# A width-31 depthwise convolution on TensorE: 8 time phases by 16 channels in the partitions instead of 4 by 32

## Chip, cores and metric

One Trainium2 chip, all 8 cores, one batch element per core. The time is the device time in microseconds (us) of the slowest core. In some executions the cores of one die show a lower granted clock (0.89 to 0.92 on one die in a run of 853.56 us) and the whole run is some per cent longer; such slow runs are left out of all comparisons. "Control" below means the kernel before, unaltered, run beside the experiments. "Core mean" is the mean of the eight core spans over the fast runs; it scatters less than the slowest core.

## The reference, cut to what matters

```python
D_MODEL = 1024; BATCH = 8; SEQ = 2048; CFM_K = 31        # FFN_HIDDEN = 2816
# per sequence: x (2048, 1024) f32, conditioning vector c (1024)
h  = modulate(rmsnorm(x, g_pre_mix), sh1, sc1)            # sh, sc, gt from silu(c) @ w_ada
gb, gc, v, a, g = split(h @ w_in, 5)                      # 512 columns each
y_short = gb * causal_dwconv(gc * v, w_short, b_short)    # width 3
u = a * sigmoid(g)                                        # (S, 512)
u = causal_dwconv(u, w_cfm_dw, b_cfm_dw)                  # depthwise, width 31   <- the change
u = layernorm(u, g_cfm_ln, b_cfm_ln)                      # over the 512 channels
y_cfm = silu(u)
y = per_head_rmsnorm(concat(y_short, y_cfm)) * beta_mix   # heads of 64 channels
x = x + gt1 * rmsnorm(y @ w_out, g_post_mix)              # output projection
x = x + gt2 * rmsnorm(swiglu(modulate(rmsnorm(x), ...)), g_post_ffn)
```

## The kernel before

The program records every operation with an estimated cost; a static scheduler then fixes the order of each engine's instructions before the run. So an engine executes in that order, even if a DMA comes later than planned and other work would be ready.

The depthwise convolution would waste TensorE if each channel had its own row of weights only. So the 128 partitions hold 32 channels times 4 time phases (position t has phase t mod 4). One 128 x 128 tap matrix then mixes all phases of a channel, and 31 taps need only 9 shifts of the phase-decimated sequence. VectorE builds the tap matrices from a table `wv` and a mask `dlt`.

```python
NPH = 4; CH = S // NPH; NG = 16; NTAP = 9; HALO = 32; URow = HALO + CH
cw_s = sb_space("cw", 4, NTAP * 128, BF16, at=xc_off)     # room for tap matrices built ahead
junk_s = sb_space("junk", 1, D, BF16)                     # scratch: squares nobody reads
xq = x_d.rearrange("(b p q) d -> q b p d", p=128, q=NPH)  # token tiles: every 4th row
...
def norm_cast(xt, i, dst):
    act(Tile(junk_s).v(), xt, AF.Square, ..., accum=sm(SM_SSQ + i), name="pn_sq")
    rsqrt_col(i, "pn_rs")                                 # two small GpSimd instructions
    return dve("tensor_scalar", ..., out=dst, in0=xt, scalar1=sm(SM_RS + i), op0=ALU.mult)
...
for g in range(NG):                                       # the convolution stage
    cw = Tile(cw_s)
    dve("tensor_tensor", ..., name "cwm")                 # 1152 elements a partition
    b = bank('mm', *B05)
    for s in range(NTAP):
        o = s * 128
        u0 = g * URow + HALO - s
        mm(b.v(), cw.v(o, o + 128), up.v(u0, u0 + CH), s == 0, s == NTAP - 1, name="conv")
    uv = u1.v(g * CH, g * CH + CH)
    act(uv, b.v(), AF.Identity, bias=..., name="cv_ev")
    act(s1, b.v(), AF.Square, bias=..., name="cv_sq")
    dve("tensor_copy", [uv], [s0], ...)                   # cast to bf16
    mm(km.v(), ones_ln.v(), s0, ...); mm(kq.v(), ones_ln.v(), s1, ...)   # LayerNorm sums
    if g % 2 == 1 and g >= 3 and g < 11: ada_cols(6 + (g - 3) // 2, ...) # conditioning pieces
    ...
def outproj(q, pairs):                                    # output projection, quarter q
    for b in range(4):
        xt = Tile(xc_s).v()                               # 4 buffers: load x, add, store x1
        dma("pool", [(xt, xq[q, b])], [], [xt], 1.35, "xload2")
        ...                                               # 16 matmuls of 512 into a PSUM pair
        post(pt.v(), xt, 0, 16 + i)                       # gate, Square into junk, root, add
        dma("sp", [(x1q[q, b], xt)], [xt], ..., "x1st")
        xb_ = Tile(xn_s)
        last = norm_cast(xt, 32 + i, xb_.v())
    to_hT(xns, q, 1, last, (6, 7))                        # transposes for the FFN
```

Of the kernel before, what the change touches and what calls it, by code (L numbers as in the profile page):

```python
# [7 lines left out]
F32 = mybir.dt.float32  # L8
BF16 = mybir.dt.bfloat16
# [9 lines left out]
NPH = 4  # L19
CH = S // NPH  # L20
NG = 16
NTAP = 9
HALO = 32
URow = HALO + CH
# [439 lines left out]
def build_program():  # L464
# [17 lines left out]
    with es:  # L482
# [24 lines left out]
        u1 = buf("u1", NG * CH, F32)  # L507
        up = buf("up", NG * URow, BF16)
        stg_s = sb_space("stg", 4, CH, BF16)
        dg3 = buf("dg3", 12 * 128, BF16)  # L510
        end_stg = cur[0]
        cvb = [buf("cvb%d" % i, 4 * URow, BF16, at=up.off + i * 8 * URow) for i in range(4)]
# [9 lines left out]
        cw_s = sb_space("cw", 4, NTAP * 128, BF16, at=xc_off)  # L522
        lnb = [buf("ln%d" % i, 512, F32, at=xc_off + 2048 * (5 + i)) for i in range(3)]
# [8 lines left out]
        junk_s = sb_space("junk", 1, D, BF16)  # L532
# [10 lines left out]
        wv = buf("wv", NW, BF16)  # L543
        dlt = buf("dlt", 32, BF16)
# [74 lines left out]
        def wload(src, n, name, sp=slot_s, split=1, **kw):  # L619
# [14 lines left out]
        dve("tensor_copy", [ident.v()], [sel.v()], 250, "c6", out=View(lambda: sel.v(0, 128, 0, 4).ap.rearrange("k (c p) -> k c p", p=4), []),  # L634
            in_=ident.t[0:4, 0:4].unsqueeze(1).to_broadcast([4, 32, 4]))
        mk = bank("tp", 6, 7)
        mm(mk.v(0, 128), sel.v(0, 128, 0, 4), sel.v(0, 128, 0, 4), True, True, n=128, name="mask")
        dve("tensor_scalar", [mk.v()], [ones_ln.v()], 250, "c7", out=ones_ln.t[:, :], in0=mk.v(0, 128), scalar1=1.0 / 512.0, scalar2=None, op0=ALU.mult)
        dve("tensor_scalar", [mk.v()], [blk32.v()], 250, "c7", out=blk32.t[:, :], in0=mk.v(0, 128), scalar1=1.0 / 64.0, scalar2=None, op0=ALU.mult)
        dve("tensor_tensor", [ident.v()], [dlt.v()], 150, "c7", out=dlt.t[:, :], in0=ident.t[:, 0:32], in1=ident.t[:, 32:64], op=ALU.add)  # L640
        for h in range(2, 4):
            dve("tensor_tensor", [ident.v(), dlt.v()], [dlt.v()], 150, "c7", out=dlt.t[:, :], in0=dlt.t[:, :], in1=ident.t[:, 32 * h:32 * h + 32], op=ALU.add)
# [24 lines left out]
        def ada_cols(piece, kind, l, half, banks, **kw):  # L667
            s = wload(wada_d[piece], 4096, "wada%d" % piece, **kw)
# [38 lines left out]

        xq = x_d.rearrange("(b p q) d -> q b p d", p=128, q=NPH)
        x1q = x1_d.rearrange("(b p q) d -> q b p d", p=128, q=NPH)
        oq = out_d.rearrange("(b p q) d -> q b p d", p=128, q=NPH)  # L710
# [7 lines left out]
        def norm_cast(xt, i, dst):  # L718
            act(Tile(junk_s).v(), xt, AF.Square, n=1024, scale=1.0 / 32.0, accum=sm(SM_SSQ + i), writes=[("ssq", i)], name="pn_sq")
            rsqrt_col(i, "pn_rs")  # L720
            return dve("tensor_scalar", [xt, ("rs", i)], [dst], 750, "pn_xn", out=dst, in0=xt, scalar1=sm(SM_RS + i), scalar2=None,
                       op0=ALU.mult)
# [73 lines left out]
        def glu(j, q, gv, av, late=""):  # L796
# [6 lines left out]
            for c in range(4):  # L803
                g = 4 * j + c
                wk += up.v(g * URow + HALO, g * URow + HALO + CH, 32 * q, 32 * q + 32).keys
            dv = upv[32 * q:32 * q + 32, 4 * j:4 * j + 4, HALO:HALO + CH]
            return dma("sp", [(dv, sv.v())], [sv.v()], [View(None, wk)], SHUF, "ushuf")
# [34 lines left out]
        for g in range(NG):  # L842
            cw = Tile(cw_s)
            ov = View(lambda cw=cw: cw.v().ap.rearrange("k (s c p) -> k s c p", s=NTAP, p=NPH), [])
            w3 = wv.t[:, g * NTAP * NPH:(g + 1) * NTAP * NPH].rearrange("k (s p) -> k s p", s=NTAP)
            dve("tensor_tensor", [wv.v(), dlt.v()], [cw.v()], 1300, "cwm", out=ov,
                in0=dlt.t[:, :].unsqueeze(1).unsqueeze(3).to_broadcast([128, NTAP, 32, NPH]),
                in1=w3.unsqueeze(2).to_broadcast([128, NTAP, 32, NPH]), op=ALU.mult)
            b = bank('mm', *B05)
            for s in range(NTAP):  # L850
                o = s * 128
                u0 = g * URow + HALO - s
                mm(b.v(), cw.v(o, o + 128), up.v(u0, u0 + CH), s == 0, s == NTAP - 1, name="conv")
            uv = u1.v(g * CH, g * CH + CH)
            act(uv, b.v(), AF.Identity, reads=[K_V], bias=vc(V_BCF + g), npt=1, name="cv_ev")
            s1 = Tile(sq_s).v()
            act(s1, b.v(), AF.Square, reads=[K_V], bias=vc(V_BCF + g), npt=1, name="cv_sq")
            s0 = Tile(sq_s).v()
            dve("tensor_copy", [uv], [s0], 430, "cv_bf", out=s0, in_=uv)
            mm(km.v(), ones_ln.v(), s0, g == 0, g == NG - 1, name="lnm")  # L860
            mm(kq.v(), ones_ln.v(), s1, g == 0, g == NG - 1, name="lnq")
            if g % 2 == 1 and g >= 3 and g < 11:
                ada_cols(6 + (g - 3) // 2, "sc" if g < 7 else "sh", 1, (g // 2 + 1) % 2, B05, split=4)
            elif g == 11:
                wb = wload(wb_d, 4096, "wb", split=4)
                rowb(0)
                rg0 = [rowg(0, half) for half in range(2)]
        mv, rv, m2 = tmean.v(), trstd.v(), lnb[2].v()
        act(mv, km.v(), AF.Copy, name="ln_m")
        dve("tensor_tensor", [mv], [m2], 690, "ln_m2", out=m2, in0=mv, in1=mv, op=ALU.mult)  # L870
        dve("tensor_tensor", [kq.v(), m2], [rv], 690, "ln_var", out=rv, in0=kq.v(), in1=m2, op=ALU.subtract)
        act(rv, rv, AF.Ln, reads=[("eps",)], bias=sm(SM_EPS), npt=1, name="ln_ln")
        act(rv, rv, AF.Exp, scale=-0.5, name="ln_exp")

        last_silu = [None]

        def ln(g):
            uv = u1.v(g * CH, g * CH + CH)
            dve("tensor_tensor", [uv, mv], [uv], 690, "ln_sub", out=uv, in0=uv, in1=mv, op=ALU.subtract)
            dve("tensor_tensor", [uv, rv], [uv], 690, "ln_mul", out=uv, in0=uv, in1=rv, op=ALU.mult)  # L880
            last_silu[0] = act(uv, uv, AF.Silu, reads=[K_V], bias=vc(V_BLN + g), scale=vc(V_GLN + g), npt=2, name="silu")

        def head_norm(h):
            st = pair('hd', 6)
            for h2 in range(2):
                for gg in range(2):
                    g = 2 * (h + h2) + gg
# [3 lines left out]
                    mm(st.v(h2 * 512, h2 * 512 + 512, part=h2), blk32.v(), s1, gg == 0, gg == 1, name="hdst")  # L891
# [3 lines left out]
            for h2 in range(2):  # L895
                for gg in range(2):
                    g = 2 * (h + h2) + gg
                    uv = u1.v(g * CH, g * CH + CH)
                    sv = Tile(ystg_s)
                    r2 = rr.v(h2 * 512, h2 * 512 + 512)  # L900
                    dve("scalar_tensor_tensor", [uv, r2, K_V], [sv.v()], 750, "hd_out", out=sv.v(), in0=uv, scalar=vc(V_BETC + g), in1=r2,
                        op0=ALU.mult, op1=ALU.mult)
# [5 lines left out]
                    dv = yT.t[32 * c:32 * c + 32, (4 + j) * S:(5 + j) * S].rearrange("c (p t) -> c p t", p=NPH)  # L908
                    dma("sp", [(dv, sv.v())], [sv.v()], [View(None, wk)], SHUF, "yshuf")

        behind = {i: [lambda g=g: ln(g) for g in range(2 * i, 2 * i + 2)] for i in range(8)}
        for i in range(4):
            behind[8 + 2 * i] = [lambda h=h: head_norm(h) for h in (2 * i,)]

        for i in range(4):
            hk = []
            for q in range(4):
# [249 lines left out]
```

## Time and profile before

| | kernel before |
|---|---|
| median of 4 runs | 803.19 us (one of the four slow) |
| profiled run | 801.97 us; core spans 789.9 to 800.4 us |
| TensorE busy, slowest core | 746.4 of 800.4 us |
| convolution stage | 42 us, all TensorE |

The profiled core shown is core 5, the slowest. The groups of the convolution by form, kernel before. Columns: line, engine, operation, output<-input with shapes, count, then busy us and mean ns of one, then idle time of that engine just before and what ended most of it:

```profile
L576 PE MATMUL ps<-up,cw 128*128 128x512 bf16 x144 | 33.9, 379 | 0.0
...
L592 DVE TENSOR_TENSOR cw<-dlt,wv 128x1152 bf16<-128x1152 bf16 x16 | 21.7, 1356 | 8.1 <-PE ps L576 8.1
...
L588 ACT ACTIVATE u<-ps,vt 128x512 f32<-128x512 f32 x16 | 11.0, 687 | 21.7 <-PE ps L576 21.7
```

TensorE has no idle time before its 144 convolution matmuls; VectorE and ScalarE wait for TensorE, not the other way round.

### The profile page before, as it was taken

How to read it: one execution, taken by the hardware profiler on the slowest of the kernel's cores; microseconds unless marked ns; L12 is line 12 of the kernel's file. 1: busy time of each engine (PE TensorE's matmuls, PEld its weight loads, DVE VectorE, ACT ScalarE, POOL GpSimd, SP SyncE). 2: the span in 40 equal slices, each digit the busy share in tenths (PEclk: the TensorE clock that was granted, in tenths of full speed). 3: DMA queues.
4: the chain of work that ended last, by engine and by line, in shares of the span. 5: the costliest groups of instructions: out<-in, count | busy, mean ns of one | idle time of the engine just before them, and what ended most of it. 6: DMA issues, size and time to landing. Idle time of an engine off the chain costs nothing.

```text
span 800.4 us, 10695 instructions; the slowest of 8 cores (789.9 to 800.4 us)
## 1 busy us (share of the span) xinstructions
PE 746.4 (93%) x3969; PEld 349.7 (44%) x3969; DVE 298.0 (37%) x429; ACT 261.0 (33%) x413; POOL 139.5 (17%) x275
## 2 busy tenths in 40 slices
PE   0788999999999989799999999999999999999993
PEld 0444444544444434354444444444444444444441
DVE  4226556584557566454122221222212221212221
ACT  3327344677566754344111110111211111101110
POOL 8024142210302225333100000000000000000000
PEclk9999999999999999989999999999999999999997
DMA  8996199924994478979995567333334432002311
GB/s 178 218 172 214 52 152 150 178 35 88 172 217 122 84 219 193 195 161 211 180 159 118 102 95 146 105 110 119 98 69 77 82 65 41 1 1 92 118 54 52
DMA packets 32051, 97.91 MB, mean 122 GB/s; under 512 B 3584, under 2 KB 7936, under 8 KB 28672
## 3 DMA queue, kind: packets, MB, share of 16 engines
q0 software_dynamic: 20048, 66.74, 45.9%
q1 hardware_dynamic: 11952, 30.49, 11.7%
q8 instruction: 32, 0.52, 0.3%
q14 instruction: 19, 0.16, 0.1%
HBM read 125.15 MB, written 16.78 MB: 177 GB/s over the span
## 4 chain that ended last, share of the span: by engine, by line
PE 80%; DMA 10%; POOL 3%; issue 2%; DVE 2%; ACT 2%; POOLq 0%; DVEq 0%; ACTq 0%; SPq 0%
PE ps L576 79%; DMA xa<-x 6%; DMA x1s<-xc 3%; DMA xc<-x 2%; POOL small L596 1%; ACT junk L588 1%; PE ps L741 1%; DVE xc L592 1%; POOL slot L608 1%; DVE pga L592 0%; POOL xa L608 0%; POOL wdn L608 0%; DVE xn L592 0%; POOL wag L608 0%; ACT hT L588 0%
## 5 line engine op out<-in xcount | busy, mean ns | idle before, releaser
L576 PE MATMUL ps<-hT,slot 128*128 128x512 bf16 x1792 | 394.6, 379 | 0.6 <-DVE actT L592 0.6
L576 PEld LDWEIGHTS ps<-hT,slot 128*128 128x128 bf16 x1792 | 174.8, 98 | 210.6 <-issue 2.1
L576 PE MATMUL ps<-wdn,actT 128*128 128x512 bf16 x704 | 152.3, 379 | 0.0
L592 DVE TENSOR_TENSOR actT<-ev,ps 128x512 bf16<-128x512 f32 x88 | 60.5, 687 | 205.6 <-PE ps L576 204.9
L588 ACT ACTIVATE ev<-ps 128x512 f32<-128x512 f32 x88 | 52.4, 596 | 217.0 <-PE ps L576 217.0
L576 PEld LDWEIGHTS ps<-wdn,actT 128*128 128x128 bf16 x704 | 68.9, 98 | 83.0
L588 ACT ACTIVATE junk<-ps 128x1024 bf16<-128x1024 f32 x32 | 32.7, 1023 | 148.2 <-DVE pgb L592 141.4
L596 POOL TENSOR_SCALAR small<-small 128x1 f32<-128x1 f32 x64 | 19.4, 303 | 304.8 <-ACT junk L588 303.4
L576 PE MATMUL ps<-hT,wag 128*128 128x512 bf16 x256 | 60.7, 394 | 7.3 <-DMA wag<-wag 5.7
L576 PE MATMUL ps<-wo,yT 128*128 128x512 bf16 x256 | 60.1, 384 | 1.8 <-ACT ev L588 1.2
L592 DVE TENSOR_TENSOR pgb<-ps,gtg 128x1024 f32<-128x1024 f32 x16 | 19.6, 1225 | 80.5 <-PE ps L576 80.5
L608 POOL DMA_DIRECT2D slot<-wgu x22 | 12.2, 552 | 190.5 <-PE ps L576 185.5
L741 PE MATMUL ps<-ident,xn 128*128 128x128 bf16 x256 | 19.7, 236 | 26.9 <-DVE xn L592 25.1
L576 PEld LDWEIGHTS ps<-hT,wag 128*128 128x128 bf16 x256 | 24.9, 101 | 38.4 <-issue 13.3
L596 POOL TENSOR_TENSOR small<-small 128x1 f32<-128x1 f32 x64 | 40.0, 625 | 8.8 <-POOL small L596 0.4
L576 PEld LDWEIGHTS ps<-wo,yT 128*128 128x128 bf16 x256 | 25.0, 99 | 32.4 <-issue 5.6
L588 ACT ACTIVATE ev<-ps,small 128x512 f32<-128x512 f32 x44 | 29.7, 680 | 25.4 <-PE ps L576 22.1
L592 DVE SCALAR_TENSOR_TENSOR xc<-pgb,small,xc 128x1024 f32<-128x1024 f32 x16 | 20.5, 1284 | 37.4 <-POOL small L596 37.4
L576 PE MATMUL ps<-up,cw 128*128 128x512 bf16 x144 | 33.9, 379 | 0.0
L608 POOL DMA_DIRECT2D slot<-wada x36 | 19.5, 583 | 77.1 <-PE ps L576 77.0
L741 PEld LDWEIGHTS ps<-ident,xn 128*128 128x128 bf16 x256 | 17.4, 106 | 31.7 <-issue 30.5
L588 ACT ACTIVATE hT<-ps,small 128x512 bf16<-128x512 bf16 x32 | 21.7, 729 | 27.0 <-PE ps L741 14.6
(91 smaller groups left out, 486.6 us busy)
## 6 DMA issues: line engine op xcount, KB each, us to landing
slot<-wgu POOLq DMA_DIRECT2D x22, 1024.0 KB, 12.7
slot<-wada POOLq DMA_DIRECT2D x32, 256.0 KB, 14.2
xc<-x POOLq DMA_DIRECT2D x16, 512.0 KB, 12.0
x1s<-xc SPq DMA_DIRECT2D x16, 512.0 KB, 8.1
xc<-x1s SPq DMA_DIRECT2D x16, 512.0 KB, 4.1
out<-xc SPq DMA_DIRECT2D x16, 512.0 KB, 2.6
xa<-x POOLq DMA_DIRECT2D x14, 512.0 KB, 31.0
wdn<-wdn POOLq DMA_DIRECT2D x22, 256.0 KB, 13.1
```

Source lines behind the costliest of these rows:

```text
L576: return P.op("pe", lambda e: e.matmul(out.ap, lhsT=lhsT.ap, rhs=rhs.ap, start=start, stop=stop), reads=[lhsT, rhs] + list(reads), writes= ...
L588: return P.op("act", lambda e: e.activation(out=out.ap, in_=in_.ap, **a), reads=[in_] + list(reads), writes=[out] + list(writes), cost=c, ...
L592: return P.op("dve", lambda e: getattr(e, meth)(**{k: val(v) for k, v in kw.items()}), reads=reads, writes=writes, cost=cost, lat=80.0, na ...
L596: return P.op("pool", lambda e: getattr(e, meth)(*a, **kw), reads=reads, writes=writes, cost=cost, lat=80.0, name=name)
L608: return [e.dma_start(out=val(o_), in_=val(i_)) for o_, i_ in pairs]
L741: P.op("pe", lambda e, ov=ov, iv=iv: e.transpose(out=ov.ap, in_=iv.ap, identity=ident.t[:, :]), reads=[iv, ident.v()], writes=[ov], cost=6 ...
```

## The change

The intent: 8 phases by 16 channels. A tap matrix of 128 x 128 then covers 8 x 8 phase pairs, so 31 taps need 5 shifts instead of 9, each over 256 columns in 32 groups instead of 512 in 16. The columns through TensorE fall from 16 x 9 x 512 = 73,728 to 32 x 5 x 256 = 40,960. Everything that depends on the layout follows: twice the shuffle DMAs at half the row length, evictions in halves (the bias differs per 16 channels), head norms over four heads at once, and rows taken 8 apart. Besides that, four of the conditioning pieces (and the weights `wb` and gate rows loaded behind them) are used in the projection stage instead of the convolution stage, six tap matrices may be built ahead instead of four, and the scratch `junk` is gone: squares are written into the tile that the normalised value overwrites.

The core of the diff (cut where "..." stands; constants of layout in other places follow the same pattern):

```diff
-NPH = 4
-CH = S // NPH
-NG = 16
-NTAP = 9
-HALO = 32
+NPH = 8
+PT = S // NPH
+CH = 2 * PT
+NC = 128 // NPH
+NG = 512 // NC
+NTAP = 5
+HALO = 4
...
-        cw_s = sb_space("cw", 4, NTAP * 128, BF16, at=xc_off)
+        cw_s = sb_space("cw", 6, 2 * NTAP * 128, BF16, at=xc_off)
...
-        junk_s = sb_space("junk", 1, D, BF16)
...
-        xq = x_d.rearrange("(b p q) d -> q b p d", p=128, q=NPH)
+        def tiles(d):
+            v = d.rearrange("(b p r) d -> r b p d", p=128, r=NPH)
+            return {(q, b): v[2 * q + b // 2, b % 2] for q in range(4) for b in range(4)}
...
-            act(Tile(junk_s).v(), xt, AF.Square, ..., name="pn_sq")
+            act(dst, xt, AF.Square, ..., name="pn_sq")
...
-            dv = upv[32 * q:32 * q + 32, 4 * j:4 * j + 4, HALO:HALO + CH]
-            return dma("sp", [(dv, sv.v())], ...)
+            for i in range(2):
+                r = NC * (2 * q + i)
+                prs.append((upv[r:r + NC, 8 * j:8 * j + 8, HALO:HALO + PT], sv.v(i * PT, i * PT + PT)))
+            return dma("sp", prs, ...)
...
-            for s in range(NTAP):
-                o = s * 128
-                u0 = g * URow + HALO - s
-                mm(b.v(), cw.v(o, o + 128), up.v(u0, u0 + CH), s == 0, s == NTAP - 1, name="conv")
+            for i in range(2):
+                for s in range(NTAP):
+                    o = (i * NTAP + s) * 128
+                    u0 = (2 * g + i) * URow + HALO - s
+                    mm(b.v(i * PT, i * PT + PT), cw.v(o, o + 128), up.v(u0, u0 + PT), s == 0, s == NTAP - 1, n=PT, name="conv")
...
-            act(uv, b.v(), AF.Identity, reads=[K_V], bias=vc(V_BCF + g), npt=1, name="cv_ev")
+            for i in range(2):
+                act(u1.v(g * CH + i * PT, g * CH + i * PT + PT), b.v(i * PT, i * PT + PT), AF.Identity, n=PT, ..., name="cv_ev")
...
-            if g % 2 == 1 and g >= 3 and g < 11:
-                ada_cols(6 + (g - 3) // 2, "sc" if g < 7 else "sh", 1, (g // 2 + 1) % 2, B05, split=4)
+            if g in (3, 5):
+                sa.append(wload(wada_d[6 + (g - 3) // 2], ...))
...
+                if j == 0 and q == 1:
+                    for h in range(2):
+                        ada_cols(6 + h, "sc", 1, h, B05, s=sa[h])
+                    for h in range(2):
+                        ada_cols(8 + h, "sh", 1, h, B05, split=4)
...
-                post(pt.v(), xt, 0, 16 + i)
+                xb_ = Tile(xn_s)
+                post(pt.v(), xt, 0, 16 + i, xb_.v())
                 dma("sp", [(x1q[q, b], xt)], [xt], [("x1d", i)], 1.95, "x1st")
-                xb_ = Tile(xn_s)
...
-                dma("pool", [(xt, xq[q, b])], [], [xt], 1.35, "xload2")
+                dma("pool", [(xt, xq[q, b])], [], [xt], 1.35, "xload2", after=yops if (q, b) == (0, 0) else ())
```

The last line makes the first x load of the output projection wait for the shuffles of the convolution's result.

## The prediction

> **What bounds the kernel now.** I read the page first, then the core spans, the waits of TensorE, the table of windows and last the timeline of the convolution stage.
>
> ```profile
> PE 746.4 (93%) x3969; PEld 349.7 (44%) x3969; DVE 298.0 (37%) x429; ACT 261.0 (33%) x413; POOL 139.5 (17%) x275
> PE   0788999999999989799999999999999999999993
> DMA  8996199924994478979995567333334432002311
> ```
>
> TensorE is busy for 93% of the span, and the row of slices has holes only in its first four slices, around slice 14 to 17 (280 to 374 us) and at the end. VectorE, ScalarE and the DMA engines are full in single stretches only. The windows say where:
>
> ```profile
> 30.00:73.00 43.00, 36.78 (x288) 17.94 (x288) 13.89 (x24) 19.34 (x34) 11.37 (x20) 0.96 0.99 232
> 106.00:148.00 42.00, 42.00 (x330) 20.93 (x328) 24.35 (x39) 20.23 (x32) 11.53 (x22) 1.00 1.02 154
> 280.00:374.00 94.00, 85.12 (x451) 40.65 (x450) 52.15 (x60) 43.09 (x73) 35.45 (x72) 0.96 0.85 198
> 374.00:787.00 413.00, 413.00 (x1919) 187.22 (x1915) 92.91 (x111) 62.66 (x107) 26.35 (x57) 1.00 0.43 93
> ```
>
> (Columns: window, its length, then busy time and count of PE, PEld, DVE, ACT and POOL, then granted clock, DMA share, GB/s.) The convolution stage, 106 to 148 us, is 42.00 of 42.00 us TensorE: whatever comes off TensorE there comes off the span, if no other engine takes its place. The 413 us of FFN are full too and are not touched. The view of waits for TensorE lists what little idle time there is:
>
> ```profile
> PE ps L741 <- DVE xn L592: 25.1, 4, 17.3
> PE ps L576 <- DMA wag<-wag: 5.7, 2, 4.1
> ...
> PE ps L576 <- ACT ev L588: 1.2, 1, 1.2
> ```
>
> 17.3 us of the first is the start, which the change leaves alone. Another 6.1 us is one stall at 340 us, on the core shown; the same line has only 18.1 to 21.9 on the others, so that stall is the slowest core's bad luck with a late store.
>
> **How long a matmul holds TensorE.** A mean of 379 ns for 512 columns is a latency that includes the pipeline. The rate comes from differences of starts:
>
> ```profile
> 106.08 4.49 PE L576 MATMUL ps<-up,cw 128*128 128x512 bf16 x20
> 110.40 0.59 PE L576 MATMUL ps<-sq,ones_ln 128*128 128x512 bf16 x2
> ...
> 127.04 0.94 PE L576 MATMUL ps<-cact,slot 128*128 128x1 bf16 x32
> 127.85 1.24 PE L576 MATMUL ps<-up,cw 128*128 128x512 bf16 x5
> ```
>
> 110.40 minus 106.08 over 20 is 216 ns for 512 columns. 127.85 minus 127.04 over 32 is 25 ns for one column with its own weight load. Transposes, 128 columns with a load each, start 8 in 0.445 us, 55.6 ns. The line through 128 and 512 columns has 0.418 ns a column and 2.1 ns fixed, so a 256-column matmul should take 109 ns. The 25 ns case shows that the load of 128 weights doesn't stand in the way of it.
>
> **What the Trainium skill says.** "TensorE: Matmul & The Clock Gate", section "Wait — 56ns, not 53.3ns?", gives N / 2.4 GHz plus about 2.5 ns for back-to-back matmuls and a floor of about 25 ns: the trace agrees (216, 55.6, 25). Its section "Back-to-back issue gap" gives 81 ns for real streams of load and matmul at N = 128; this trace has 55.6 with loads, and I use the trace. "VectorE: DVE Perf Modes", section on the TRN2 errata, puts a fixed cost on each VectorE and ScalarE instruction, so two halves cost more than a whole; the trace has 597 and 1056 ns for plain ScalarE passes of 512 and 1024, about 0.9 ns an element, and a fixed part of about 140 ns in these durations. "DMA: Bandwidth & Descriptors", section "Specifications", wants at least 512 B a transfer for line rate; the new shuffles have exactly that, against 1 KB now. No run yet shows shuffles of 512 B.
>
> **The change, part by part.** The causal width-31 convolution is done by interleaving time phases with channels in the 128 partitions: 4 phases by 32 channels now, 8 by 16 then. A tap matrix mixes all phases, so 9 shifts of 512 columns in 16 groups become 5 shifts of 256 columns in 32 groups.
> 1. Convolution matmuls. Now 144 x 216 ns = 31.1 us. Then 32 x 5 = 160 x 109 ns = 17.4 us. Gain 13.7 us, all on the path by the window above.
> 2. LayerNorm statistics and head norms: the same columns in twice the matmuls; 48 matmuls of 512 become 96 of 256. 48 x 2.1 ns: +0.1 us. The short convolution gains four instructions, nothing. TensorE sum: -13.6 us.
> 3. Four conditioning pieces (32 single-column matmuls each, 0.81 us) move from the convolution stage into the projection stage. Both are TensorE-bound: zero, but the convolution stage alone should shrink from 42 to about 24.4 + 0.8 (bias) = 25 us: 17.4 + 64 x 109 ns = 24.4.
> 4. VectorE builds the tap matrices: 1280 instead of 1152 elements each, and starts in the timeline are 1.28 us apart now, so about 1.41 us. With the cast (0.35 us) a pair of groups needs 1.76 us of VectorE against 24.4/16 = 1.53 us of TensorE. VectorE would be the bound but for the six matrices (four now) built ahead in its idle time; 10 x 1.41 + 16 x 0.35 = 19.7 us then stand against 24.4. It fits.
> 5. ScalarE evicts in two halves for the bias per 16 channels: 687 ns becomes twice about 460, and starts about 0.35 us apart; with a square of about 0.52 that is 1.24 us a pair, under 1.53. SiLU halves add about 16 x 0.35 = 5.5 us over the projection stage, where ScalarE is not the bound (23.80 of 32 us just now), and the head norms drop four of their eight passes of 1.1 us. Beside TensorE: zero.
> 6. The shared scratch for squares goes; they are written into the normalised tile's own buffer. So a square must now wait for one of four such buffers, which the transposes of the four tiles before it free. At a boundary between quarters of the output projection this could hold the PSUM pair some 3 us longer (estimate: transposes end 11.4 us after a quarter's last projection by the chain of durations, the square comes at about 8). Gate/up matmuls fill TensorE there; 0 to 3 us lost, I take 0.5.
> 7. Shuffles: 16 + 16 DMAs become 32 + 32 of half size, issued by SP at 0.55 us each. The one at risk is the last into the convolution's input: three of them landed at a median of 7.7 us, against 3.0 us when the queues are quiet, because the weight loads fill the DMA there (1.02). The last starts at 107.3 us. At double descriptors, say 14 us, it lands at 121; the faster convolution needs that quarter of the channels at 106 + 12 x 1.53 = 124.4, against 137 now. It just holds. I take 0.7 us for it.
> 8. Bigger tap table (1280 instead of 576 columns): about 2 us of DMA at the start, behind the loads TensorE waits for. Zero.
>
> Sum: -13.6 + 0.5 + 0.7 is about -12.5 to -13. From 803.2: 790.
>
> **The rivals.** (a) The convolution stage becomes bound by its feeders: VectorE's tap matrices or late shuffles. For: 1.76 against 1.53 us a pair, and a reserve of only 3 us on the last shuffle. Against: six matrices ahead. It would show as TensorE waiting on the tile cw or up and give back 3 to 7 us: 793 to 797. (b) The loss of the scratch and the new static order hurt the output projection, 280 to 374 us, where 9 us are already idle and the order is fixed before the run: a DMA later than planned stalls TensorE. For: that 6.1 us stall is of this kind. Against: fill matmuls are plenty. 793 to 800. (c) The opposite: the slowest core's 6.1 us stall goes away in the new order. Then 783 to 786, which is over 2%. (d) 256-column matmuls are not half of 512 because loads come through: at 130 ns each the 160 would be 20.8 us, and the 96 small ones another 2 us worse: 796. The 55.6 ns of the transposes speak against it.
>
> **Range and chances.** The TensorE sum is firm to a microsecond, the losses are one-sided, the stalls of the slowest core can move by some 5 us either way. So 790, range 783 to 798. Over 2% faster means under 787.1, 3 us more than the sum gives and only with (c): 0.27. Slower by 2% needs a gain turned into a loss of 30 us: 0.01.
>
> **What would show it.** Right: 160 convolution matmuls of 256 columns starting 109 ns apart with no idle time of note before them; a convolution stage of about 25 us; the FFN stretch still 413 us; TensorE busy for some 13 us less in all. Step 4 is wrong if TensorE waits on cw, step 7 if it waits on up, step 6 if idle time between the short convolution and the FFN exceeds 9 us. The prediction fails upward if these together pass 8 us, downward if idle time that the change doesn't aim at shrinks.

## The result, and the profile after

| | before | after |
|---|---|---|
| median | 802.00 us (15 runs, 798.13 to 937.21) | 783.38 us (10 runs, 782.22 to 853.56) |
| ratio of fast runs, 95% interval | | 0.9773 [0.9752, 0.9794] |
| profiled run: core spans | 789.9 to 800.4 us | 775.6 to 781.3 us |
| profiled run: TensorE busy / not busy, slowest core | 746.4 / 54.0 us | 733.2 / 48.1 us |

The kernel is faster by 2.3%. The medians count slow runs too (two of the 15, one of the 10); the ratios don't. A ratio here is the mean time of one kernel's fast runs over that of the other's of the same rounds, so it is not quite the ratio of the medians. The prediction of 790.0 was 6.6 us too high; the result lies just inside its range, at the low edge, and in the class that had been given 0.27.

On the slowest cores the span fell by 800.4 - 781.3 = 19.1 us: 13.2 us is TensorE time and 5.9 us is idle time of TensorE. The first is the change's aim; the second was not predicted.

The page of the kernel after (slowest is core 6) has this row of 40 slices for TensorE:

```profile
PE   0779999999999999999999999999999999999993
```

The dip that the kernel before had in slices 14 to 16 is gone. The table of windows, kernel after, with the prediction's columns:

```profile
107.30:131.90 24.60, 24.60 (x250) 21.85 (x249) 20.38 (x30) 20.68 (x47) 3.40 (x7) 1.00 1.07 162
...
269.00:359.00 90.00, 87.13 (x450) 40.79 (x448) 50.84 (x58) 41.28 (x70) 34.36 (x73) 1.00 0.86 206
359.00:768.00 409.00, 409.00 (x1919) 186.08 (x1917) 94.25 (x114) 64.00 (x109) 25.64 (x56) 1.00 0.42 94
```

The convolution stage is 24.60 us, all of it TensorE, where it had been 42. The FFN is full in both kernels and runs the same 1919 matmuls: the windows are 409 and 413 us only because I cut them by eye. In the output-projection stretch TensorE is idle for 90.00 - 87.13 = 2.9 us; before it was 94.00 - 85.12 = 8.9 us.

The groups of the convolution by form, kernel after:

```profile
L579 PE MATMUL ps<-up,cw 128*128 128x256 bf16 x160 | 21.1, 272 | 0.0
...
L595 DVE TENSOR_TENSOR cw<-dlt,wv 128x1280 bf16<-128x1280 bf16 x16 | 23.6, 1482 | 0.2 <-PE ps L579 0.2
...
L591 ACT ACTIVATE u<-ps,vt 128x256 f32<-128x256 f32 x32 | 14.6, 468 | 4.6 <-PE ps L579 4.6
```

There is no idle time before the 160 matmuls. VectorE's wait on TensorE before building a tap matrix has shrunk from 8.1 to 0.2 us: it now builds them at its own pace. The waits of TensorE, kernel after (columns: total us, count, longest):

```profile
PE ps L747 <- DVE xn L595: 17.6, 2, 17.3
PE ps L579 <- DMA wag<-wag: 7.4, 2, 5.7
PE ps L579 <- ACT ev L591: 1.2, 1, 1.2
PE ps L579 <- DMA slot<-wada: 0.8, 2, 0.6
```

No wait on the tiles `cw` or `up`. The wait on `xn` has lost its 6.1 us stall, and 17.3 of the 17.6 us is the start as before. The 0.8 us on the conditioning weights `wada` are new in their place, the projection stage at 153 and 160 us; the kernel before waited 1.6 us for such weights, at the start.

**The stall that vanished.** On core 5 of the kernel before, TensorE's timeline around it (start us, length, engine and line, operation, count, and in brackets the idle time before it with what ended it):

```profile
340.39 1.86 PE L741 MATMUL ps<-ident,xn 128*128 128x128 bf16 x16 [6.12 <-DVE xn L592]
```

and the two instructions that lead there, from GpSimd's and VectorE's timelines of the same core:

```profile
331.64 0.59 POOL L608 DMA_DIRECT2D xc<-x  x1 [8.21 <-DMA x1s<-xc]
...
334.42 0.75 DVE L592 TENSOR_SCALAR xn<-xc,small 128x1024 bf16<-128x1024 f32 x1 [7.22 <-POOL small L596]
```

Read backwards: TensorE wants to transpose `xn`; VectorE, which makes it, has waited 7.22 us for `small`, the reciprocal root that GpSimd computes; GpSimd stood for 8.21 us in front of an x load it had to issue, because the buffer `xc` was still being stored by an earlier `x1s` store. The roots come behind that load in GpSimd's fixed order. Between that `xn` and the last one of the quarter, for which TensorE waits, lie one more addition, square and root. The windows around the stall show a second cost. The clock is the second number from the end but two, 0.77 and 0.50:

```profile
334.20:340.30 6.10, 0.07 (x1) 0.00 (x0) 4.07 (x5) 2.26 (x4) 2.45 (x6) 0.77 0.99 204
340.30:343.70 3.40, 3.31 (x20) 2.28 (x21) 1.88 (x4) 1.44 (x2) 2.24 (x5) 0.50 0.43 88
```

For 3.4 us after the stall TensorE works at half clock: about 1.7 us more.

**Is it only one core's luck?** I had called it the slowest core's bad luck. So I added up TensorE's idle time after 262 us for all eight cores:

| profiled run | idle after 262 us, mean of 8 cores | idle at the start (before 110 us), mean |
|---|---|---|
| before | 5.0 us | 29.9 us |
| after | 1.6 us | 31.2 us |

Every core of the kernel before loses 2.6 to 8.7 us there. This is a property of the kernel, not of one core. (1.2 us of each figure is one wait for `ev` before the first projection tile, which every run has; the rest are stalls.)

The static order of the two kernels differs in that stretch, in two ways. First, inside a quarter 14 gate/up matmuls of the FFN separate two projection tiles before, so that a tile comes every 6.48 us; after, there are 16, and a tile comes every 6.90 us. Second, the boundary of two quarters. TensorE's timeline there, before and then after (`ident,xn` are transposes, `wo` is a tile of the output projection, `hT,slot` are gate/up matmuls):

```profile
306.85 1.05 PE L741 MATMUL ps<-ident,xn 128*128 128x128 bf16 x16
307.74 1.67 PE L576 MATMUL ps<-wo,yT 128*128 128x512 bf16 x7
309.25 1.06 PE L741 MATMUL ps<-ident,xn 128*128 128x128 bf16 x16
```

```profile
328.91 1.06 PE L747 MATMUL ps<-ident,xn 128*128 128x128 bf16 x16
329.81 1.67 PE L579 MATMUL ps<-hT,slot 128*128 128x512 bf16 x7
331.32 1.06 PE L747 MATMUL ps<-ident,xn 128*128 128x128 bf16 x16
```

Before, the next quarter's first projection tile begins between the two sets of transposes; after, gate/up matmuls stand there and the projection comes later. I first took the slower pace for the cure, as it gives the x loads and x1 stores, which share four buffers, more time. The runs a_late and b_late below speak against the pace.

### The profile page after: what moved, and what is told of

It is laid out like the page before. It is cut to its first block, busy times and chain, and to the rows that moved or that the text cites. A ratio compares the mean times of both kernels' runs of the same rounds, so it can differ in the third digit from the quotient of the medians.

```text
span 781.3 us, 10955 instructions; the slowest of 8 cores (775.6 to 781.3 us)
## 1 busy us (share of the span) xinstructions
PE 733.2 (94%) x4037; PEld 356.0 (46%) x4037; DVE 300.5 (38%) x449; ACT 261.6 (33%) x441; POOL 133.5 (17%) x275
## 4 chain that ended last, share of the span: by engine, by line
PE 85%; DMA 9%; POOL 2%; DVE 1%; issue 1%; ACT 1%; POOLq 0%; DVEq 0%; ACTq 0%; SPq 0%
PE ps L579 84%; DMA wag<-wag 5%; DMA slot<-wada 2%; DMA xc<-x 2%; PE ps L747 1%; DMA x1s<-xc 1%; POOL slot L611 1%; POOL xa L611 0%; ACT xn L591 0%; DVE xc L595 0%; POOL small L599 0%; ACT hT L591 0%; DVE cw L595 0%; DVE xn L595 0%; DVE pgb L595 0%
## 5 line engine op out<-in xcount | busy, mean ns | idle before, releaser
L591 ACT ACTIVATE xn<-ps 128x1024 bf16<-128x1024 f32 x32 | 32.7, 1022 | 143.9 <-DVE pgb L595 141.4
L579 PE MATMUL ps<-hT,wag 128*128 128x512 bf16 x256 | 63.2, 406 | 9.4 <-DMA wag<-wag 7.4
L599 POOL TENSOR_SCALAR small<-small 128x1 f32<-128x1 f32 x64 | 16.3, 255 | 305.4 <-ACT xn L591 303.9
L579 PEld LDWEIGHTS ps<-hT,wag 128*128 128x128 bf16 x256 | 25.7, 103 | 41.9 <-issue 18.1
L591 ACT ACTIVATE ev<-ps,small 128x512 f32<-128x512 f32 x44 | 29.9, 681 | 34.3 <-PE ps L579 34.0
L747 PE MATMUL ps<-ident,xn 128*128 128x128 bf16 x256 | 19.2, 230 | 19.4 <-DVE xn L595 17.6
L591 ACT ACTIVATE xn<-xc 128x1024 bf16<-128x1024 f32 x16 | 16.9, 1057 | 38.2 <-DVE xc L595 38.1
```

Of the source, the lines that this page charges most:

```text
L579: return P.op("pe", lambda e: e.matmul(out.ap, lhsT=lhsT.ap, rhs=rhs.ap, start=start, stop=stop), reads=[lhsT, rhs] + list(reads), writes= ...
L591: return P.op("act", lambda e: e.activation(out=out.ap, in_=in_.ap, **a), reads=[in_] + list(reads), writes=[out] + list(writes), cost=c, ...
L599: return P.op("pool", lambda e: getattr(e, meth)(*a, **kw), reads=reads, writes=writes, cost=cost, lat=80.0, name=name)
L747: P.op("pe", lambda e, ov=ov, iv=iv: e.transpose(out=ov.ap, in_=iv.ap, identity=ident.t[:, :]), reads=[iv, ident.v()], writes=[ov], cost=6 ...
```

## The experiments

The open questions were: how much of the gain is TensorE columns; what removed the idle time of the output projection; whether the feeders of the convolution have real reserve. Ratios are against the kernel before in the same job. Because the control's own interval is about 0.35% wide to each side, I rank the small effects by core mean and TensorE idle time also.

### The columns alone: b_5shifts

The kernel before with only 5 of its 9 shifts, all else alike. Its output is wrong, which doesn't matter for the time. (Relative error 0.146.)

```diff
-            for s in range(NTAP):
+            for s in range(5):
...
-                mm(b.v(), cw.v(o, o + 128), up.v(u0, u0 + CH), s == 0, s == NTAP - 1, name="conv")
+                mm(b.v(), cw.v(o, o + 128), up.v(u0, u0 + CH), s == 0, s == 4, name="conv")
```

> Wrong on purpose: the kernel before with only the first 5 of its 9 shift matmuls of 512 columns in each of 16 groups; everything else stays, so 64 matmuls of 216 ns are missing, 13.8 us, as many columns' time as the change saves (13.7). GpSimd's order in the output projection stays that of before. Theory A: exactly this time goes and the stall stays: 801.5 - 13.8 = 787-789, ratio 0.982 to 0.985. Theory B (the stall goes because the stage comes 13 us earlier): 780-783, ratio about 0.975. If the convolution stage is held by another engine, less than 13.8 us goes.

Measured: 788.97 us median, ratio 0.9806 [0.9773, 0.9839]; mean time 15.4 us less and core mean 14.5 us less. 64 matmuls of 216 ns are 13.8 us. So the columns taken off TensorE come off the time, and alone give most of what the change gives. The idle time after 262 us stayed at 4.4 us: fewer columns do not cure the stalls.

### The scratch, from both sides: b_xn, a_junk, a_junk2

b_xn is the kernel before with squares written into the normalised tile; a_junk and a_junk2 (the same edit, repeated in another job) are the changed kernel with the scratch back. The tap table `wv` then had to move onto a buffer used later, for lack of room.

```diff
# b_xn (against before); a_junk and a_junk2 do the reverse in the changed kernel
-            act(Tile(junk_s).v(), xt, AF.Square, ..., name="pn_sq")
+            act(dst, xt, AF.Square, ..., name="pn_sq")
...
-                post(pt.v(), xt, 0, 16 + i)
+                xb_ = Tile(xn_s)
+                post(pt.v(), xt, 0, 16 + i, xb_.v())
```

> The kernel before with one part of the change alone: the square's throw-away result goes into the normalised tile's own buffer, the separate scratch is gone. No other edit. The convolution stays at 9 shifts of 512 columns. Its GpSimd stream then has the order of the changed kernel in the output projection (four reciprocal-root pairs ahead of the next x load that waits for a store), the kernel before has two. Theory A (the 6 us beyond the predicted gain come from this order: in the kernel before a load that waits 8.2 us for a store blocks the roots queued behind it on GpSimd): TensorE's wait for xn in the output projection goes, mean core span 795 to about 791, time 801.5 to 794-797, ratio 0.990 to 0.994. Theory B (the stall goes away because of the other row stride of the tiles, or because the stage comes earlier): ratio 0.998 to 1.006.

> The changed kernel with the scratch for the squares put back (the tap table lies where the gate vector is loaded later, to make room); GpSimd's order in the output projection is then that of the kernel before. Theory A: the stall of TensorE on xn between 300 and 345 us comes back on some cores, 1 to 6 us by core, time 783.4 to 787-791, ratio to before 0.982 to 0.987. Theory B: stays at 782-785, ratio 0.976 to 0.979.

> The variant of the changed kernel with the separate scratch put back, once more, now on the same chip as the unaltered changed kernel. If the scratch's removal and the order it brings are worth something: 1 to 4 us more than the changed kernel, with 1 to 3 us more TensorE idle time in the output projection. If all of the gain is the convolution's columns: within 1 us of it.

| run | median | ratio [95%] | idle after 262 us |
|---|---|---|---|
| b_xn | 800.62 | 0.9958 [0.9928, 0.9987] | 2.1 us |
| a_junk | 787.04 | 0.9791 [0.9758, 0.9823] | 3.3 us |
| a_junk2 | 787.77 | 0.9782 [0.9752, 0.9812] | 3.3 us |
| a_again2 (after, unaltered, job of a_junk2) | 786.92 | 0.9770 [0.9735, 0.9804] | 1.8 us |

b_xn's ratio lies between the ranges of its two theories and a_junk's at the edge of theory B, so the times alone decide nothing; a_junk2 is within the 1 us that was said for "only columns" in time, but not in idle time. In both kernels the version without the scratch has the lower idle time: 2.1 against 4.5 (control) to 5.0 us, and 1.6 to 1.9 against 3.3. In time it is 3.3 us in the kernel before and about 1 us in the kernel after (mean time and core mean of a_junk2 against a_again2: +1.0 and +0.9). I had expected the loss of the scratch to cost up to 3 us. Its sign is wrong. The edit changes the order too: b_xn has the changed kernel's pace and boundary (15 or 16 gate/up matmuls between projection tiles, gate/up between the transposes), and a_junk and a_junk2 have those of the kernel before. So these runs test scratch and order together.

b_xn still has a stall, on core 3, and its length is of interest (timeline of TensorE, then the windows, both core 3):

```profile
327.88 5.30 PE L575 MATMUL ps<-wo,yT 128*128 128x512 bf16 x16 [2.36 <-ACT xn L587]
```

```profile
327.80:331.20 3.40, 3.32 (x8) 1.16 (x9) 2.30 (x3) 0.64 (x1) 0.97 (x2) 0.52 0.85 236
```

A gap of 2.36 us was enough for half clock in the next 3.4 us, and 16 matmuls took 5.30 instead of 3.62 us. So this short stall cost (2.36 + 1.68) / 2.36 = 1.7 times its length. What this projection matmul waited for is ScalarE's square, which reads the PSUM pair that the matmul needs and writes into `xn`. It isn't the wait of step 6, though: that square started at 326.63 us, right behind another square that had waited 6.5 us for VectorE's addition, and that addition came after a root that GpSimd computed late: it had stood for 8.39 us before an x load, because of a store of `x1`. It is the chain of above once more. Nor does such a wait need the new buffer: TensorE waits for squares in the kernels with the scratch too (`junk`, 0.8 us on the mean core before and in the control, against 0.3 in b_xn and 0.05 after).

### The row stride: b_stride8

The kernel before with its token tiles taken 8 rows apart, as in the changed kernel. Its output is wrong, which doesn't matter for the time. (Relative error 0.36: the phases no longer fit.)

```diff
-        xq = x_d.rearrange("(b p q) d -> q b p d", p=128, q=NPH)
+        def tiles(d):
+            v = d.rearrange("(b p r) d -> r b p d", p=128, r=8)
+            return {(q, b): v[2 * q + b // 2, b % 2] for q in range(4) for b in range(4)}
...
+        xq, x1q, oq = tiles(x_d), tiles(x1_d), tiles(out_d)
```

> Wrong on purpose: the kernel before, with the tokens of x, of the stored middle stream and of the output taken at the stride of 8 rows of the changed kernel instead of 4; no instruction and no order differs. Theory A: the stride does nothing for the stall: ratio 0.998 to 1.003, and TensorE's wait for xn stays. Theory B: stores land sooner, the stall goes: 0.990 to 0.994. It also tells whether the stride makes the start later (waits for the first projection weights 5.5 us on the mean of the cores before, 6.6 after).

Measured: 800.39 us, ratio 0.9953 [0.9922, 0.9984], once more between the two ranges; idle after 262 us 2.3 us. No instruction's shape or count changes in this run, and still half of the idle time goes. What the kept traces show is that stores landed sooner, as theory B had it: between 262 and 375 us a store of `x1` took 6.8 us on the mean of all cores and 10.6 at most, against 8.4 and 21.4 in the control and 7.6 and 13.0 in the kernel before. Why rows farther apart land sooner I can't say. So there are at least two parts of the change that each lower the idle time, and each gives a gain in time of 0.4 to 0.5%, little more than the control's scatter.

### Is it GpSimd's queue? b_late, a_late

The chain above suggests that x loads block the roots in GpSimd's queue because the scheduler believes that stores land early. So the scheduler was told that a store of `x1` lands 8 us later. This changes only the order of instructions.

```diff
-                o.done = ring[e] + 1300.0
+                o.done = ring[e] + 1300.0 + (LATE if o.name == "x1st" else 0.0)
+LATE = 8000.0
```

> The kernel before with the same number altered: no data, buffer or instruction differs from it, only the static order in the output projection (GpSimd's root pairs ahead of the x loads that wait for stores). Theory A: TensorE's wait for xn at the boundary of quarters goes, mean core span down 3 to 4 us, time down 4 to 7, ratio 0.991 to 0.995. Theory B: 0.998 to 1.004, with the wait still there.

> The changed kernel with one number in its build-time scheduler altered: the store of the middle stream is assumed to land 8 us later. Same instructions, another static order in the output projection alone, with more root pairs ahead of each x load on GpSimd. Theory A (order on GpSimd sets the stalls): 0 to 2 us less than the unaltered changed kernel, ratio to it 0.997 to 1.000. Theory B (the order has no part): equal within 0.15%, or slower because the x loads start later.

b_late: 799.15 us, ratio 0.9962 [0.9934, 0.999]. GpSimd's waits for stores fell to between 0 and 0.8 us a core, from 6 to 15 us in the control. Yet TensorE's idle time after 262 us remained 3.9 us (control 4.5), and 8.8 us on core 5; its wait for `xn` halved (1.2 against 2.3 us on the mean core), and other waits grew. Where it went, from the waits between 262 and 375 us on core 5 of b_late, and that core's timeline of VectorE:

```profile
DVE xc L592 <- DMA xc<-x: 12.3, 4, 5.0
...
PE ps L741 <- DVE xn L592: 4.2, 3, 2.4
```

```profile
335.81 1.28 DVE L592 SCALAR_TENSOR_TENSOR xc<-pga,small,xc 128x1024 f32<-128x1024 f32 x1 [3.57 <-DMA xc<-x]
```

The load of x is no longer in the way of the roots, but now it comes later, and VectorE's addition waits for the load itself. I read this as a limit under the queue: four buffers `xc` each go through load, addition and store, and taking one wait away moves it along that cycle. No run isolates that. The DMA engines are busy in this stretch (0.85 of the time in the kernel before, 0.99 around its stall), but 0.86 in the changed kernel too, so their share alone doesn't make the stalls. The ratio lies between the two ranges. My theory that GpSimd's order alone makes the stalls has fallen.

a_late: 785.17 us, 0.979 [0.9763, 0.9817], beside the unaltered changed kernel at 0.981 in the same job; idle 1.65 against 1.9 us. No difference that the intervals could show.

The two runs also test the pace, as the scheduler changed it in one quarter of each. TensorE's timeline, a_late (core 2) and then b_late (core 5):

```profile
316.86 3.18 PE L579 MATMUL ps<-hT,slot 128*128 128x512 bf16 x14
```

```profile
328.41 3.62 PE L576 MATMUL ps<-hT,slot 128*128 128x512 bf16 x16
```

a_late's projection tiles come every 6.48 us there, no stall follows that quarter, and its eight cores idle as little as those of the changed kernel; b_late's come every 6.91 us, and at the end of that quarter core 5 stalls for 2.38 us. So the slower pace isn't what helps. The boundary fits better: the kernels with gate/up matmuls between the transposes (the changed kernel three times, a_late, a_cw2, b_xn) are idle for 1.4 to 2.1 us, the others for 3.3 to 5.0 us, but for b_stride8 with 2.3 us. That is a pattern over the runs; none changes the boundary alone.

### Is it the scatter of the stores? b_x1c

The kernel before, with the intermediate stream `x1` stored in contiguous rows rather than 4 apart.

```diff
-        x1q = x1_d.rearrange("(b p q) d -> q b p d", p=128, q=NPH)
+        x1q = x1_d.rearrange("(q b p) d -> q b p d", p=128, q=4)
```

> The kernel before with the middle stream stored in HBM as 16 contiguous blocks of 512 KB instead of rows at a stride of 4; right result, same order, x and output untouched. The wrong-on-purpose run with stride 8 gained 0.5% against the expectation. If that came from how the middle stream's rows lie, contiguous blocks change it too: 0.990 to 0.997. If it came from the reads of x, or is chance: 0.998 to 1.002.

Measured: 799.70 us, ratio 0.9974 [0.9949, 0.9999], idle 4.1 us against 4.5 in the control. It matters little for the idle time. The ratio lies between the two ranges. So if the stride acts, it isn't through the stores of `x1` alone.

### The reserve of tap matrices: a_cw2

The changed kernel with room for 2 tap matrices instead of 6.

```diff
-        cw_s = sb_space("cw", 6, 2 * NTAP * 128, BF16, at=xc_off)
+        cw_s = sb_space("cw", 2, 2 * NTAP * 128, BF16, at=xc_off)
```

> The changed kernel with room for 2 tap matrices instead of 6. By the prediction's step 4: VectorE needs 1.74 us a pair of groups (measured starts) against 1.53 of TensorE; with 2 ahead the last matrix is ready 1.1 + 14 x 1.74 = 25.5 us after the stage starts, and TensorE wants it at 15 x 1.53 = 23.0: TensorE waits about 2.5 us on cw in the stage, which is then bound by VectorE, and the time is 2 to 3 us above the changed kernel. If the loads are hidden in another way: no wait.

Measured: 789.54 us, ratio 0.9798 [0.9757, 0.984]; against a_again2 in the same job +2.4 us in mean time and +1.75 us in core mean. TensorE's timeline, core 0:

```profile
112.68 0.60 PE L579 MATMUL ps<-up,cw 128*128 128x256 bf16 x4 [0.73 <-DVE cw L595]
...
130.30 1.04 PE L579 MATMUL ps<-up,cw 128*128 128x256 bf16 x8
...
131.97 1.04 PE L579 MATMUL ps<-up,cw 128*128 128x256 bf16 x8
...
133.81 1.04 PE L579 MATMUL ps<-up,cw 128*128 128x256 bf16 x8
```

Groups now start 1.67 and 1.84 us apart, in the mean over five of them 1.75 us: the pace of VectorE, 1.76 us a pair in step 4. The stage takes 30.3 us instead of 24.6. But the time grew by only 2.4 us, because, as the order shows, the scheduler had filled most of the gaps with single-column bias and conditioning matmuls from later stages. The list of waits shows almost nothing on `cw` (0.7 us), and 2.5 us on weights of those early-pulled matmuls instead. A stage that is bound by another engine need not show as waits on that engine's tile.

### The yardstick: b_again, a_again, a_again2

The two kernels, unaltered, run as if they were experiments.

> The kernel before, unaltered, run as if it were a change: the control. Four variants of it that alter only order, scratch or row addresses have each come out 0.3 to 0.5% faster, which looks too alike. If the yardstick is even: ratio 0.998 to 1.002 and equal mean core spans, and those gains are real. If it is uneven (or those gains are chance): 0.995 to 0.998, and none of them counts.

> The changed kernel once more, unaltered, as the yardstick on this chip for the three beside it: ratio to before 0.975 to 0.979, mean core span 778 to 780.

> The changed kernel unaltered, for the third time, beside its variant with the scratch put back on one chip. 0.977 and 0.981 so far on two chips: 0.976 to 0.982, mean core span 15 to 16 us under the kernel before.

| run | median | ratio [95%] | core mean against before | idle after 262 us |
|---|---|---|---|---|
| b_again | 804.54 | 0.9983 [0.9948, 1.0019] | -0.4 us | 4.5 us |
| a_again | 787.25 | 0.9810 [0.9781, 0.9839] | -14.9 us | 1.9 us |
| a_again2 | 786.92 | 0.9770 [0.9735, 0.9804] | -16.1 us | 1.8 us |

b_again shows that the comparison is even and that effects below some 0.35% can't be read from one job's times. The changed kernel gave 0.977, 0.981 and 0.977 in three jobs: a gain of 15 to 18 us.

By core mean the small variants of the kernel before gained 2.9 us (b_xn), 3.3 (b_stride8), 2.4 (b_late) and 1.8 (b_x1c), against 0.4 of the control. Their idle time after 262 us fell by 2.4, 2.2, 0.5 and 0.4 us (one profile each). So the idle time accounts for the first two at most; what b_late and b_x1c gained is open.

Not run: the changed kernel without the gate on the first x load (`after=yops`), with the conditioning pieces back in the convolution stage, with the order of the quarters' boundary changed alone, or with x loads issued from SP. No version tried is clearly faster than the changed kernel.

## Why the prediction was right and wrong

**Steps 1 and 2, the columns: right.** Predicted 109 ns for a 256-column matmul. TensorE's timeline, kernel after:

```profile
107.35 3.78 PE L579 MATMUL ps<-up,cw 128*128 128x256 bf16 x33
110.97 0.60 PE L579 MATMUL ps<-sq,ones_ln 128*128 128x256 bf16 x4
```

33 starts lie in 110.97 - 107.35 = 3.62 us, 109.7 ns each. The whole is then 160 x 109.7 ns = 17.6 us. Busy time fell by 13.2 us on the slowest cores against -13.6 predicted, and b_5shifts shows that such time is on the path. Rival (d), 130 ns, is refuted.

**Step 3, the moved pieces: nearly right.** The convolution stage is 24.6 us where "25" stood. In the projection stage TensorE waits 0.58 + 0.21 us for the weights of these pieces instead of nothing.

**Step 4 and rival (a), VectorE: right.** VectorE's timeline, kernel after, starts of two tap matrices with one cast between them:

```profile
110.46 1.48 DVE L595 TENSOR_TENSOR cw<-dlt,wv 128x1280 bf16<-128x1280 bf16 x1
...
112.20 1.48 DVE L595 TENSOR_TENSOR cw<-dlt,wv 128x1280 bf16<-128x1280 bf16 x1
```

That is 1.74 us a pair, predicted 1.76, and TensorE didn't wait for it. a_cw2 shows that this is owed to the matrices built ahead. Step 5 holds too: 468 ns for a half eviction where "about 460" stood, and no wait.

**Step 7, the shuffles: the loss of 0.7 us did not come.** The shuffles into `up` landed after up to 11.1 us (8.3 before; 14 estimated) on the slowest cores, and TensorE waited for none. Step 8 and the start: the slowest cores' wait for the first weights `wag` grew from 5.7 to 7.4 us, and idle time before 110 us grew by 1.3 us in the first pair of runs (29.9 to 31.2), by 2.4 us in a later pair (30.6 to 33.0). I had booked zero. No run isolates why. Profiles whose start is that of the kernel before scatter from 29.9 to 31.5 us, those with the start of the changed kernel from 31.2 to 33.1; b_stride8 has 31.3, so the row stride alone doesn't make it later; b_xn, where only the squares are written elsewhere, has 32.7, and with the scratch put back it is still 32.2 and 32.4. So the tap table is not needed for a late start, and how much is scatter stays open.

**Step 6: wrong in its sign.** I read the idle time of the output projection as bad luck of one core and added 0.5 us for the loss of the scratch. In truth every core lost time there (mean 5.0 us, 4.5 in the control) and the changed kernel loses 1.6 to 1.9 us. Rival (c) had this outcome, but for a smaller reason: not one stall on one core but some 3 us on the mean core. What the runs show of the cause is: writing squares into the normalised tile halves the idle time in the kernel before (b_xn), and putting the scratch back nearly doubles it in the kernel after (3.3 twice); the row stride of 8 halves it too (b_stride8); fewer columns (b_5shifts), a later x load (b_late) and contiguous stores (b_x1c) do not cure it. The wait that step 6 feared, a square held up by the transposes, was not seen: the one case (b_xn, core 3) goes back to a late store. The scheduler puts gate/up matmuls where that wait would have been, as step 6 said it could. Taking the scratch away also changed the static order, and the pace of projection tiles isn't what helps in it (a_late, b_late); the boundary of quarters fits all runs but b_stride8 and was not tested alone. The shares of order and stride stay open, and why stores land sooner at the larger stride does too.

**The sum.** The prediction's own terms give -13.6 + 0.5 + 0.7 = -12.4, which is 790.8 from 803.2; 790 was a little more than the sum gave. For the mean core of the profiled runs TensorE's working time fell by 14.5 us (746.6 to 732.1: the span without the gaps above 150 ns and without the 13.25 us after its last matmul), its idle time in the output projection by 3.4, while the start grew by 1.3 and other waits by 0.4: together -16.2 us. Measured: 794.9 to 778.6, -16.3. Of the 14.5, 13.6 are the columns; the 0.9 left may be the half clock after stalls, which after 262 us took 0.85 us a core before and nothing after, but earlier the clock lost some 0.6 us more, so I have not separated it.

The slowest core gains 0.2 to 2.3 us more than the mean, by the job, because the spread of the cores narrows (slowest minus mean 5.5 us before in its one profile, 3.3 us after over the fast runs; 4.5 and 6.1 against 4.2 and 3.9 in the later jobs). So 790 was 6.6 us high. 1.2 us of that is the starting point: 15 runs of the kernel before have a median of 802.0, the 4 I had 803.2. The gain was 18.6 us where I had 13.2. Against the sum of 12.4 these are 6.2 us more: step 6 is 3.9 (3.4 gained, 0.5 booked as lost), step 7 is 0.7, working time 0.9, the narrower spread some 2.3, and the start and other waits take 1.7 back, together 6.1. That the range held is luck: 783.4 is 0.4 us above its end, and it held because of an outcome that had been argued as one core's chance. The chance of 0.27 for "faster" rested on (c) being one core's chance event. The view of waits on the other seven cores had spoken against that: 18.1 to 21.9 us on the line, less some 17.3 of start, leaves 0.8 to 4.6 us of stall on each, and I read past it.

## What to carry to other kernels

When a stage is all TensorE, count columns: a layout that packs more useful taps into each 128 x 128 matrix pays in full, so long as the engines that feed it have worked ahead. Add up idle time over all cores and for a whole stretch before calling a stall one core's luck, because a fixed instruction order turns late DMAs into stalls on all of them. And where a wait vanishes after a change of order only, look where it went: in b_late it moved from GpSimd to VectorE, and TensorE stood nearly as long as before (3.9 against 4.5 us).

## What the Trainium skill lacked or had wrong

- "TensorE: Matmul & The Clock Gate", section "Wait — 56ns, not 53.3ns?": its N / 2.4 GHz + 2.5 ns gives 109.2 ns for N = 256; the trace has 109.7, so it holds between the sizes that the trace of the kernel before had shown. Its section "Back-to-back issue gap" gives 81 ns for load-and-matmul streams at N = 128 and 131 ns at N = 512; here these took 55.6 (transposes, each with its load) and 216 ns.
- The same page, section "What's actually happening", on the clock gate's states: half clock "after ≥1 idle window (~3.4µs)". Here a gap of 2.36 us (b_xn, core 3) was followed by 3.4 us at a granted clock of 0.52, while gaps of 2.33 us (a_junk, core 7) and 2.83 us (b_5shifts, core 2) had no such effect. So of gaps below the page's 3.4 us, one of 2.36 us was enough and one of 2.83 us was not. The page says there that the window is free-running; these traces don't show where it begins.
- The same page, section "Seeing it yourself", has a peak-current limit of 13/16 once three cores of a die run dense matmuls, held while the load lasts. Here the mean granted clock of fast runs is 0.98 to 0.99 with all eight cores at it. The limit does appear, but for a short time: in b_again the clock of core 0 is 1.00 from 145 to 160 us, 0.81 from 161 to 175 and 1.00 from 176 to 190, with TensorE busy for 99% of each stretch; four of the 14 profiles have such a stretch, of 15 us at most. Slow runs come lower in the mean (0.89 to 0.92 on one die in the 853.56 us run, 0.84 to 0.85 in a run of 923.62 us).
- "DMA: Bandwidth & Descriptors", section "Specifications" asks for 512 B a transfer: shuffles of 512 B into `up` landed in 2.6 us in the median and 11.1 us at most, those of 1 KB in 3.0 and 8.3; into `yT` it was 4.8 and 13.5 against 3.4 and 5.1 (slowest cores). No page says what such a shuffle takes beside full DMA queues.
- The same page, section "Latency and other measured facts", has a loss of rate for row pitches in HBM of 2 MiB and more against 512 KiB. It has nothing for small ones: tiles of 4 KB rows taken 32 KB instead of 16 KB apart left TensorE 2.3 instead of 4.5 us idle, and the stores landed in 6.8 instead of 8.4 us in the mean (b_stride8 against the control), so here the larger pitch did no harm and perhaps good; the cause is open.
